# Seven products for eight in six of 22 up-projection chunks of a two-layer encoder

## The chip, the cores and the metric

The kernel runs as one program on one core of a Trainium2 chip. The metric is the device time of one execution in microseconds. The kernel before has a median of 1114.0 us in three runs (1113.79 to 1115.45). The profile is of one further execution.

## What is computed

The reference is an encoder of two layers on 512 tokens of width 1024: layer 0 mixes tokens with a gated linear attention, layer 1 with softmax attention, and each mixer is followed by a gated MLP. Only the MLP is touched here:

```python
def conv_ffn(h, w_up, w_conv, b_conv, w_down):      # h: 512 x 1024, w_up: 1024 x 5632, w_down: 2816 x 1024
    u = h @ w_up
    u = lax.conv_general_dilated(u, w_conv[:, None, :], window_strides=(1,), padding=[(1, 1)], ...) + b_conv
    val, gate = jnp.split(u, 2, axis=-1)
    return (jax.nn.silu(gate) * val) @ w_down
# per layer: x = x + mixer(rmsnorm(x)); x = x + conv_ffn(rmsnorm(x), ...)
```

## The kernel before

Features lie on the 128 partitions and the 512 tokens along a row. Every fp32 matrix product is done as three products of rounded parts: a weight or an input is split into a high part (ScalarE copies it to fp32r) and a low part (VectorE subtracts the high part), and TensorE adds high x high, high x low and low x high. So one strip of weights costs a ScalarE copy into a `wh` tile and a VectorE subtraction into a `wl` tile, besides its transfer into a `raw` tile by SyncE's queue.

**The up projection** runs over 22 chunks `m` in a layer. A chunk has two output tiles (`t` = 0 for the value, 1 for the gate); each tile takes 8 blocks of the input times 3 matmuls of 128x512 from one half of the chunk's strip. `act_up` then scales the sums by the norm's row `R` (VectorE, `u<-up,R`), runs the convolution (one ScalarE and two VectorE instructions on `y` for each tile), the SiLU and the product of value and gate.

**The down projection** is done partly by seven products for eight already. `prepare` (for each two chunks) makes sums and differences of the activations' half tiles (two GpSimd subtractions, two VectorE ones) and splits them into `gu` tiles; `summed` makes the sums of weight blocks on VectorE; `down_part`, run after chunks 9 and 17, issues for each of four strips seven products of 12 matmuls of 128x256 and puts partial sums in each other's places by ScalarE copies from PSUM to PSUM. One of the four weight pieces of such a strip gets its low part by a GpSimd DMA that accumulates (`wl<-raw`, L189). The last chunks' activations are multiplied plainly (`PLAIN`).

**What sets the order.** A scheduler takes the instructions by the order in which the program writes them, and engines then run their own queues strictly in order. `Weights` makes pieces ahead of their use (`ahead`); `wh` and `wl` have 3 tiles each, `raw` has 2, and single tiles serve some pieces of the summed strips (`ring`, `sq`). The pool `g` of 22 pairs of tiles holds, in this stage, the `gu` tiles and the weights' sums.

Of the kernel before, what the change touches and what calls it, by code (L numbers as in the profile page):

```python
# [45 lines left out]
DOWN_AFTER = {9: 0, 17: 1}  # L46

# [9 lines left out]
def hybrid_encoder_kernel(  # L57
# [54 lines left out]
    class Weights:  # L112
# [7 lines left out]
        def add(self, src, strips=None, pieces=2):  # L120
            for i in strips or range(src.shape[0]):
                self.todo += [(src, i, h) for h in range(pieces)]
                if pieces > 2:
                    self.sums[id(src), i] = {}

        def make(self, key):
# [8 lines left out]
            if (id(src), i) in self.sums:  # L135
                self.made[id(src), i, h] = self.summed(self.raw[id(src), i], self.sums[id(src), i], h)
                return
# [10 lines left out]
        def summed(self, raw, sums, h):  # L148
# [3 lines left out]
            if h == 0:  # L152
                sums["e"] = e = big(F32, "sum")
                with tc.issue_after(self.last.ins) if self.last else ExitStack():
                    dve.tensor_tensor(e[:, :S], a21, a22, ALU.add)
                    dve.tensor_tensor(a21, a21, a11, ALU.add)
                r = raw[:, : 2 * S]
            elif h == 1:
                e = sums["e"]
                dve.tensor_tensor(e[:, S:], e[:, :S], a11, ALU.add)  # L160
                r = e
            elif h == 2:
                r = raw[:, 2 * S :]
            else:
                e = sums["e"]
                r = tmp("sq", "sum4")
                dve.tensor_tensor(r, e[:, S:], a12, ALU.add)
                hi, lo = (sp.tile([P, S], F32R, tag="sq", bufs=3, name=nm(n)) for n in ("wh4", "wl4"))
                act.activation(hi, r, AF.Copy)
                self.last = dve.tensor_tensor(lo, r, hi.bitcast(F32), ALU.subtract)  # L170
                return hi, lo
# [49 lines left out]

    def add_ffn(layer):
        first = 0
        for m, part in DOWN_AFTER.items():
            W.add(up[layer], range(first, m + 1))
            W.add(down_w[layer], range(part * NQ, (part + 1) * NQ), 4)
# [3 lines left out]
        W.add(up[layer], range(first, FC))  # L230
        W.add(down_w[layer], range(NPART * NQ, down_w[layer].shape[0]))
# [531 lines left out]
    def ffn(layer, norm, cw, nxt):  # L763
        w_dn = down_w[layer]

        ahead = {(m + i // 2, i % 2): n for m in DOWN_AFTER for i, n in ((-1, 2), (0, 2), (1, 5))}
        plain = {}
        down = []
        quads = {}

        def act_up(m):

            res, pss = [], []
            for t in range(2):
# [3 lines left out]
                if t == 0 and m in DOWN_AFTER:  # L778
                    down.append(down_part(DOWN_AFTER[m], m))
                    next(down[-1])  # L780
# [4 lines left out]
            for t in range(2):  # L785
                ps = pss[t]
                cc = ((layer * 2 + t) * FC + m) * 4
                w = lambda i: cw[:, cc + i : cc + i + 1]
                u = tmp("u", "u")
                dve.tensor_tensor(u, ps, norm.R, ALU.mult)  # L790
# [35 lines left out]


        PLACE = {1: (0, S), 7: (0, 0), 6: (1, S), 5: (1, 0), 2: (2, 0), 4: (2, S), 3: (3, 0)}

        def down_part(part, m):  # L830
# [3 lines left out]
            src = w_dn  # L834
            pairs = [quads.pop(part * NQ + i) for i in range(NQ)]
            st = [{} for _ in range(NQ)]
            pieces = {}

            def product(n, i, dst, start):
                h, o = PLACE[i]  # L840
                if (n, h) not in pieces:
                    pieces[n, h] = W.piece(src, part * NQ + n, h, 3)
                wh, wl = pieces[n, h]
                for j in range(NQ):
                    sl = slice(o + j * P, o + (j + 1) * P)
                    mh, ml = pairs[j][i]
                    for a, (w, m) in enumerate(((wh, mh), (wh, ml), (wl, mh))):
                        mm(dst, w[:, sl], m, start=start and j == 0 and a == 0, stop=j == NQ - 1 and a == 2,  # L848
                           skip_group_check=True)
                W.flush()  # L850

            def begin(n):
                r = st[n]
                r[1] = bank("acc", "r1")
                product(n, 1, r[1][:, :H], True)
# [5 lines left out]
            for n in range(NQ):  # L861
                r, c, d = st[n], x[2 * n], x[2 * n + 1]
                r1, r2 = r[1][:, :H], r[2][:, :H]
                product(n, 6, r2, False)
# [3 lines left out]
                product(n, 7, r4, True)  # L868
                product(n, 2, r1, False)
                product(n, 5, r2, False)  # L870
# [3 lines left out]
                product(n, 4, r3, False)  # L874
# [6 lines left out]
                product(n, 3, r2, False)  # L881
                dve.tensor_tensor(c[:, H:], c[:, H:], r2, ALU.add)
                if n == 1 and m < 2 * NQ * NPART:
                    prepare(m // 2, *late)
# [13 lines left out]
        last = late = None  # L898
        for m in range(FC):
            y = act_up(m)  # L900
            if m >= 2 * NQ * NPART:
                t = big(F32R, "gu")
                split(y, t)
                plain[m] = (t[:, :S], t[:, S:])
            elif m % 2 == 0:
                last = y
            elif m not in DOWN_AFTER:
                prepare(m // 2, last, y)
            if m in DOWN_AFTER:
                late = last, y  # L910
                for _ in down[-1]:
                    pass
        cur, open_ = None, {}
# [248 lines left out]
def _layout(inputs):  # L1162
# [53 lines left out]
    a["w_up"] = con(up.transpose(0, 4, 2, 3, 1, 5).reshape(2, FC, P, 4 * S))  # L1216
    dn = i["ffn_w_down"].reshape(2, FC, P, KC, P)
# [29 lines left out]
```

## Time and profile before

| | before |
|---|---|
| median of 3 runs | 1114.0 us |
| profiled execution: time, span | 1113.87 us, 1112.2 us |
| busy TensorE, VectorE, ScalarE, GpSimd | 1105.3, 797.4, 562.3, 117.7 us |
| granted TensorE clock | 0.999 |
| first weight load of the up projection, layer 0 and layer 1 | 225.6 us, 754.5 us after the start |

The profiled execution took 1.67 us more than its span from first to last instruction. An engine's row reads: line of the kernel, engine, operation, tile written and tiles read, their shapes, count, then busy time in all and the mean of one in ns. In rows of the timeline the first two numbers are start and duration in us. PE is TensorE, PEld its weight loads, DVE VectorE, ACT ScalarE, POOL GpSimd, SP SyncE.

### The profile page before, as it was taken

Reading aid. Unit: us, or ns where it says so; the run is one execution under the profiler, and the core shown is the slowest. Engines: PE = TensorE matmul, PEld = TensorE weight load, DVE = VectorE, ACT = ScalarE, POOL = GpSimd, SP = SyncE. Lnnn points to the kernel's source line nnn. Section 1 sums busy time; section 2 is a strip of 40 time slices with the busy share of each in tenths; the row PEclk is TensorE's granted clock in tenths of the full one; section 3 lists DMA queues with packets and bytes.
Section 4 is the critical chain, followed back from the end, with each engine's and each line's share of the span. In section 5 each row is a group of like instructions: output and inputs, shape, how many; then the busy total and the mean of one; then the engine's idle time right before and its main releaser. Section 6 shows DMA issues by size and latency. Waiting matters only on the chain.

```text
span 1112.2 us, 14752 instructions
## 1 busy us (share of the span) xinstructions
PE 1105.3 (99%) x5780; PEld 947.4 (85%) x5780; DVE 797.4 (72%) x1217; ACT 562.3 (51%) x870; POOL 117.7 (11%) x126
## 2 busy tenths in 40 slices
PE   9999999999999999999999999999999999999998
PEld 7888888888889988898888888788888998889887
DVE  6785785667889577875664578766788957797572
ACT  5565343444556444653464777644455644465340
POOL 0100122001001000100004333000100100010000
PEclk9999999999999999999999999999999999999999
DMA  6322122232226423363247765423222642336322
GB/s 230 138 89 100 71 95 77 76 114 76 76 86 175 158 76 113 98 169 114 98 128 188 177 185 154 153 76 104 86 77 81 172 164 76 114 96 168 116 76 76
DMA packets 31413, 130.52 MB, mean 117 GB/s; under 512 B 3824, under 2 KB 4336, under 8 KB 20976
## 3 DMA queue, kind: packets, MB, share of 16 engines
q1 hardware_dynamic: 21072, 102.16, 26.5%
q0 software_dynamic: 5376, 18.88, 8.5%
q10 hardware_dynamic: 4896, 8.55, 2.1%
q8 instruction: 45, 0.74, 0.3%
q14 instruction: 24, 0.20, 0.1%
HBM read 100.21 MB, written 2.10 MB: 92 GB/s over the span
## 4 chain that ended last, share of the span: by engine, by line
PE 96%; ACT 1%; DMA 1%; DVE 1%; issue 0%; POOL 0%; ACTq 0%; SPq 0%; DVEq 0%
PE r L848 14%; PE up L351 14%; PE up L350 14%; PE up L352 14%; PE op L408 8%; PE vg L382 8%; PE dn L350 2%; PE dn L352 2%; PE dn L351 2%; PE o L676 1%; PE A L350 1%; PE av L382 1%; PE A L351 1%; PE A L352 1%; PE pt L1109 1%; PE q L350 1%
## 5 line engine op out<-in xcount | busy, mean ns | idle before, releaser
L350 PE MATMUL up<-xhl,wh 128*128 128x512 f32 x704 | 274.4, 390 | 0.0
L351 PE MATMUL up<-xhl,wh 128*128 128x512 f32 x704 | 274.0, 389 | 0.0
L352 PE MATMUL up<-xhl,wl 128*128 128x512 f32 x704 | 273.9, 389 | 0.0
L199 ACT ACTIVATE wh<-raw 128x1024 fp32r<-128x1024 f32 x132 | 139.4, 1056 | 212.1 <-PE up L351 108.2
L200 DVE TENSOR_TENSOR wl<-raw,wh 128x1024 fp32r<-128x1024 f32 x132 | 161.2, 1221 | 41.0 <-ACT wh L199 40.7
L352 PEld LDWEIGHTS up<-xhl,wl 128*128 128x128 f32 x704 | 132.2, 188 | 27.5
L350 PEld LDWEIGHTS up<-xhl,wh 128*128 128x128 f32 x704 | 132.2, 188 | 27.3
L351 PEld LDWEIGHTS up<-xhl,wh 128*128 128x128 f32 x704 | 132.2, 188 | 26.9
L848 PE MATMUL r<-gu,wh 128*128 128x256 f32 x640 | 116.4, 282 | 0.0
L848 PEld LDWEIGHTS r<-gu,wh 128*128 128x128 f32 x640 | 99.7, 191 | 0.3
L790 DVE TENSOR_TENSOR u<-up,R 128x512 f32<-128x512 f32 x88 | 60.2, 686 | 54.3 <-PE up L352 54.3
L848 PE MATMUL r<-gu,wl 128*128 128x256 f32 x320 | 90.4, 283 | 0.0
L792 ACT ACTIVATE y<-u,cw 128x512 f32<-128x512 f32 x88 | 71.1, 811 | 33.2 <-DVE u L790 33.0
L382 PE MATMUL vg<-wh,xhl 128*128 128x512 f32 x256 | 80.0, 390 | 0.7 <-ACT wh L199 0.4
L408 PE MATMUL op<-oT,wh 128*128 128x512 f32 x256 | 71.8, 394 | 0.5 <-ACT p L1073 0.5
L794 DVE SCALAR_TENSOR_TENSOR y<-u,cw,y 128x511 f32<-128x511 f32 x88 | 65.8, 749 | 2.0
L793 DVE SCALAR_TENSOR_TENSOR y<-u,cw,y 128x511 f32<-128x511 f32 x88 | 65.5, 745 | 1.2 <-ACT y L792 1.2
L796 ACT ACTIVATE y<-y 128x512 f32<-128x512 f32 x44 | 27.8, 633 | 72.6 <-DVE y L794 72.4
L848 PEld LDWEIGHTS r<-gu,wl 128*128 128x128 f32 x320 | 61.1, 191 | 0.0
L189 POOL DMA_DIRECT2D wl<-raw x32 | 28.5, 890 | 299.4 <-ACT wl L142 114.7
L382 PEld LDWEIGHTS vg<-wh,xhl 128*128 128x128 f32 x256 | 47.9, 188 | 11.3 <-ACT wh L199 0.8
L408 PEld LDWEIGHTS op<-oT,wh 128*128 128x128 f32 x256 | 47.3, 188 | 11.0 <-ACT p L1073 0.9
(232 smaller groups left out, 1931.8 us busy)
## 6 DMA issues: line engine op xcount, KB each, us to landing
raw<-in_w_up_dram SPq DMA_DIRECT2D x42, 1024.0 KB, 4.9
raw<-in_w_down_dram SPq DMA_DIRECT2D x22, 1024.0 KB, 4.8
wl<-raw POOLq DMA_DIRECT2D x32, 512.0 KB, 4.6
raw<-in_w_vg_dram SPq DMA_DIRECT2D x6, 1024.0 KB, 4.8
ring<-p ACTq DMA_DIRECT2D x22, 256.0 KB, 3.1
raw<-in_w_kq_dram SPq DMA_DIRECT2D x4, 1024.0 KB, 4.8
raw<-in_w_gout_dram SPq DMA_DIRECT2D x4, 1024.0 KB, 4.9
raw<-in_w_aout_dram SPq DMA_DIRECT2D x16, 256.0 KB, 4.9
```

The lines of the kernel that those rows point to most:

```text
L199: act.activation(hi[:, sl], r[:, sl], AF.Copy)
L200: dve.tensor_tensor(lo[:, sl], r[:, sl], hi[:, sl].bitcast(F32), ALU.subtract)
L350: mm(ps, wh, mh, start=start, stop=False)
L351: mm(ps, wh, ml, start=False, stop=False)
L352: return mm(ps, wl, mh, start=False, stop=stop)
L382: mm(ps[j][:, :width], hl[k][i == 2][:, j * P : (j + 1) * P], (wl if i == 1 else wh)[:, sl], start=k == 0 and i == 0, stop=k == KC - 1 and ...
L408: mm(pss[ng][n], wt[:, sl], mv, start=k == 0 and i == 0, stop=k == KC - 1 and i == 2)
L790: dve.tensor_tensor(u, ps, norm.R, ALU.mult)
L792: act.activation(y, u, AF.Identity, scale=w(1), bias=w(3))
L793: dve.scalar_tensor_tensor(y[:, 1:], u[:, : S - 1], w(0), y[:, 1:], ALU.mult, ALU.add)
L794: dve.scalar_tensor_tensor(y[:, : S - 1], u[:, 1:], w(2), y[:, : S - 1], ALU.mult, ALU.add)
L848: mm(dst, w[:, sl], m, start=start and j == 0 and a == 0, stop=j == NQ - 1 and a == 2, skip_group_check=True)
```

## The change

Six chunks in each layer (`SEVEN`: 4, 6, 12, 14, 18 and 20) compute their two output tiles by seven products of 12 matmuls of 128x256 in the place of two tiles of 24 matmuls of 128x512. The 1024 input features are taken as four pairs of blocks, the 512 tokens as two halves, and the chunk's strip as four quarters (odd or even blocks, gate or value). The sums of the weights' quarters are made by GpSimd for these chunks (`by` is `pool`); for the down strips they stay on VectorE, but the order of the sums and their places change, so that no tile of the pool `g` is needed. `prepare_input`, once a layer and for one pair of blocks after each of the chunks 0 to 3, makes the sums of the input's half tiles and their splits. The activations of two chunks are now `held` until both are there, and `prepare` comes after a down part, not in its midst.

```diff
+SEVEN = (4, 6, 12, 14, 18, 20)
...
-        def summed(self, raw, sums, h):
+        def summed(self, raw, h, by):
             a21, a11, a12, a22 = (raw[:, n * S : (n + 1) * S] for n in range(4))
             if h == 0:
-                sums["e"] = e = big(F32, "sum")
+                r = tmp("t", "sum")
                 with tc.issue_after(self.last.ins) if self.last else ExitStack():
-                    dve.tensor_tensor(e[:, :S], a21, a22, ALU.add)
-                    dve.tensor_tensor(a21, a21, a11, ALU.add)
+                    by.tensor_tensor(r, a21, a11, ALU.add)
+                    by.tensor_tensor(a21, a21, a22, ALU.add)
+                hi, lo = pair("wh", 3, F32R, "wh"), pair("wl", 3, F32R, "wl")
+                for sl, y in ((slice(0, S), r), (slice(S, 2 * S), a11)):
+                    act.activation(hi[:, sl], y, AF.Copy)
+                    dve.tensor_tensor(lo[:, sl], y, hi[:, sl].bitcast(F32), ALU.subtract)
+                return hi, lo
+            if h == 1:
+                by.tensor_tensor(a11, a21, a11, ALU.add)
...
             else:
-                dve.tensor_tensor(r, e[:, S:], a12, ALU.add)
+                by.tensor_tensor(r, a11, a12, ALU.add)
...
+    def add_up(layer, chunks):
+        for m in chunks:
+            W.add(up[layer], (m,), 4 if m in SEVEN else 2, pool)
...
+        ahead.update({(m - 1, t): 2 for m in SEVEN for t in range(2)})
...
+        def seven_up(m):
+            pieces = {}
+            go = lambda *a: product(pieces, up[layer], m, inputs, *a)
+            r1, r2 = (bank("acc", n)[:, :H] for n in ("r1", "r2"))
+            go(1, r1, True)
+            act.activation(r2, r1, AF.Copy)
+            r4 = bank("pt", "r4")[:, :H]
+            go(7, r4, True)
+            go(6, r2, False)
+            r3 = bank("s", "r3")[:, :H]
+            act.activation(r3, r2, AF.Copy)
+            go(2, r1, False)
+            go(5, r2, False)
+            c, d = tmp("u", "u"), tmp("u", "u")
+            act.activation(d[:, H:], r2, AF.Copy)
+            dve.tensor_tensor(c[:, :H], r1, norm.R[:, :H], ALU.mult)
+            go(4, r3, False)
+            dve.tensor_tensor(d[:, H:], d[:, H:], r4, ALU.add)
+            go(3, r2, False)
+            act.activation(d[:, :H], r3, AF.Copy)
+            dve.tensor_tensor(d[:, :H], d[:, :H], r4, ALU.add)
+            dve.tensor_tensor(c[:, H:], r2, norm.R[:, H:], ALU.mult)
+            yield c
+            dve.scalar_tensor_tensor(d, d, -1.0, norm.R, ALU.mult, ALU.mult)
+            yield d
...
+        def prepare_input(p):
+            y1, y2, q = (tmp("t", n) for n in ("x1", "x2", "q"))
+            for i, y in enumerate((y1, y2)):
+                act.activation(y, x[2 * p + i], AF.Copy, scale=norm.weight(2 * p + i))
+            b11, b12, b21, b22 = y1[:, :H], y1[:, H:], y2[:, :H], y2[:, H:]
+            pool.tensor_tensor(q[:, :H], b22, b12, ALU.subtract)
+            pool.tensor_tensor(b12, b11, b12, ALU.subtract)
+            t = [big(F32R, "xt") for _ in range(2)]
+            split(b12, t[0], 0, H)
+            dve.scalar_tensor_tensor(q[:, H:], b12, -1.0, b22, ALU.mult, ALU.subtract)
+            split(q, t[1])
+            dve.scalar_tensor_tensor(b21, q[:, H:], -1.0, b21, ALU.mult, ALU.subtract)
+            split(b21, t[0], H, H)
...
-                if n == 1 and m < 2 * NQ * NPART:
-                    prepare(m // 2, *late)
...
+        held = []
         for m in range(FC):
+            held.append(act_up(m))
+            if m < KC // 2:
+                prepare_input(m)
             if m in DOWN_AFTER:
                 for _ in down[-1]:
                     pass
+            if m % 2 == 0:
+                continue
+            if m < 2 * NQ * NPART:
+                prepare(m // 2, *held)
...
+            held = []
```

How the instructions move is seen at three places of layer 0. The first is GpSimd's queue over chunks 10 to 15. Before, it holds the two subtractions of `prepare` for each two chunks (`q` and `y`) and nothing between them:

```order
L810 TENSOR_TENSOR q_3470<-y_3458,y_3384 128x256
L811 TENSOR_TENSOR y_3384<-y_3384 128x256
L810 TENSOR_TENSOR q_3634<-y_3622,y_3548 128x256
L811 TENSOR_TENSOR y_3548<-y_3548 128x256
L810 TENSOR_TENSOR q_3799<-y_3787,y_3713 128x256
```

Now the same queue, from the last of chunk 12's weight sums on (`raw_3599` is chunk 12's strip, `raw_3797` chunk 14's; `y_3582` and `y_3665` are the activations of chunks 10 and 11):

```order
L172 TENSOR_TENSOR sum_3699<-raw_3599 128x512
L194 DMA wl_3696<-raw_3599 128x1024
L866 TENSOR_TENSOR q_3677<-y_3665,y_3582 128x256
L158 TENSOR_TENSOR sum_3799<-raw_3797 128x512
L867 TENSOR_TENSOR y_3582<-y_3582 128x256
L159 TENSOR_TENSOR raw_3797<-raw_3797 128x512
L166 TENSOR_TENSOR raw_3797<-raw_3797 128x512
L172 TENSOR_TENSOR sum_3925<-raw_3797 128x512
L194 DMA wl_3922<-raw_3797 128x1024
```

Four sums of 128x512 and one DMA have come in for each of the six chunks, and the first sum for chunk 14 stands between the two subtractions of `prepare` for chunks 10 and 11.

The second place is ScalarE's queue while TensorE runs chunk 12. Before (`gu` tiles are splits of `prepare`, `wh` tiles weight strips for later chunks):

```order
L792 ACTIVATE y_3464<-u_3462,cw 128x512
L796 ACTIVATE y_3464<-y_3464 128x512
L803 ACTIVATE gu_3474<-y_3458 128x512
L199 ACTIVATE wh_3561<-raw_3516 128x1024
L803 ACTIVATE gu_3473<-y_3384 128x512
L803 ACTIVATE gu_3475<-q_3470 128x512
```

Now (`r_3693`, `r_3694`, `r_3750` are chunk 12's PSUM banks r1, r2, r3; `u_3781` its second result):

```order
L848 ACTIVATE y_3671<-u_3669,cw 128x512
L820 ACTIVATE r_3694<-r_3693 128x256
L204 ACTIVATE wh_3752<-raw_3732 128x1024
L852 ACTIVATE y_3671<-y_3671 128x512
L825 ACTIVATE r_3750<-r_3694 128x256
L859 ACTIVATE gu_3681<-y_3665 128x512
L859 ACTIVATE gu_3680<-y_3582 128x512
L829 ACTIVATE u_3781<-r_3694 128x256
L859 ACTIVATE gu_3682<-q_3677 128x512
```

Copies on which TensorE's next product waits (L820, L825, L829) now stand between instructions that wait for VectorE and GpSimd (`gu_3680` for the subtraction into `y_3582`).

The third is TensorE's queue in chunk 4, the first of the six. Before, a tile is 24 rows of one kind:

```order
L350 MATMUL up_2373<-xhl_1811,wh_2345 128x512
L351 MATMUL up_2373<-xhl_1811,wh_2345 128x512
L352 MATMUL up_2373<-xhl_1811,wl_2346 128x512
L350 MATMUL up_2373<-xhl_1817,wh_2345 128x512
L351 MATMUL up_2373<-xhl_1817,wh_2345 128x512
```

Now, where the products 7 (`r_2447`), 6 (`r_2422`) and 2 (`r_2421`) meet (`xt_2396` is the transformed input of the last pair of blocks, `up_2562` the first tile of chunk 5):

```order
L810 MATMUL r_2421<-xhl_1917,wl_2424 128x256
L810 MATMUL r_2447<-xt_2396,wh_2315 128x256
L810 MATMUL r_2422<-xt_2396,ring_2347 128x256
L810 MATMUL r_2421<-xhl_1991,wh_2423 128x256 x2
L810 MATMUL r_2421<-xhl_1991,wl_2424 128x256
L361 MATMUL up_2562<-xhl_1811,wl_2463 128x512
L359 MATMUL up_2562<-xhl_1817,wh_2462 128x512
L810 MATMUL r_2447<-xt_2396,wh_2315 128x256
L810 MATMUL r_2447<-xt_2396,wl_2316 128x256
L810 MATMUL r_2422<-xt_2396,ring_2347 128x256 x2
```

The last pair's part of products 7 and 6 stands behind most of product 2, and nine matmuls of chunk 5 stand within chunk 4. In layer 1 the three queues have the same order at these places.

More of the change, by code (lines that the diff above doesn't have):

```diff
@@ L135, in make @@
             if (id(src), i) in self.sums:
[L136 removed]
+                self.made[id(src), i, h] = self.summed(self.raw[id(src), i], h, self.sums[id(src), i])
                 return
@@ L224, in add_ffn @@
         for m, part in DOWN_AFTER.items():
-            W.add(up[layer], range(first, m + 1))
-            W.add(down_w[layer], range(part * NQ, (part + 1) * NQ), 4)
+            add_up(layer, range(first, m + 1))
+            W.add(down_w[layer], range(part * NQ, (part + 1) * NQ), 4, dve)
             at = len(W.todo) - 4 * NQ - 1
@@ L229, in add_ffn @@
             first = m + 1
-        W.add(up[layer], range(first, FC))
+        add_up(layer, range(first, FC))
         W.add(down_w[layer], range(NPART * NQ, down_w[layer].shape[0]))
```

94 lines of the change are left out of this document (47 added, 47 removed).

## The prediction

> **What bounds the kernel now.** I read the page first: who is busy, and whose work the chain that ended last consists of.
>
> ```profile
> PE 1105.3 (99%) x5780; PEld 947.4 (85%) x5780; DVE 797.4 (72%) x1217; ACT 562.3 (51%) x870; POOL 117.7 (11%) x126
> PE 96%; ACT 1%; DMA 1%; DVE 1%; issue 0%; POOL 0%; ACTq 0%; SPq 0%; DVEq 0%
> ```
>
> TensorE has hardly any idle time, and 96% of the chain is its own work, so fewer matmul cycles shorten the span if nobody else comes late. How near the others are is asked by stage: the table of windows gives, for each stretch, the busy time of PE, PEld, DVE, ACT and POOL.
>
> ```profile
> 270.20:292.00 21.80, 21.80 (x98) 18.06 (x97) 17.06 (x24) 10.57 (x14) 1.83 (x2) 1.00 0.27 100
> 398.20:420.00 21.80, 21.80 (x98) 18.06 (x97) 17.10 (x25) 10.61 (x15) 1.83 (x2) 1.00 0.26 89
> 337.60:376.30 38.70, 38.70 (x326) 38.70 (x325) 32.92 (x53) 23.78 (x35) 4.98 (x5) 1.00 0.60 172
> 503.50:525.30 21.80, 21.80 (x98) 18.04 (x97) 12.41 (x16) 6.74 (x9) 0.00 (x0) 1.00 0.25 82
> ```
>
> Two plain chunks take 21.8 us, of which VectorE is busy 17.1 us: 4.7 us are free. Late chunks (from 503.5) leave it 9.4 us.
>
> **What goes: TensorE.** A matmul's own row is longer than its pitch, since matmuls overlap; so I take the pitch from runs of one shape in the chain, 128x512 first, 128x256 second.
>
> ```profile
> 84.06 16.32 PE vg L382 x72
> 337.63 38.69 PE r L848 x324
> ```
>
> 16.32/72 = 0.227 us and 38.69/324 = 0.119 us. A plain chunk is 48 x 0.227 = 10.88 us (the 21.8 us of the windows for two), a chunk of seven products 84 x 0.119 = 10.03 us. Half of 0.227 is 0.113, so the smaller matmul gives back 5% of the 12.5%. The gain is **0.85 us a chunk, 5.1 us a layer, 10.2 us in all**: small against any wait.
>
> **What comes: VectorE, ScalarE, GpSimd.** Groups by shape, mean ns before the last bar:
>
> ```profile
> L200 DVE TENSOR_TENSOR wl<-raw,wh 128x1024 fp32r<-128x1024 f32 x132 | 161.2, 1221 | 41.0 <-ACT wh L199 40.7
> L790 DVE TENSOR_TENSOR u<-up,R 128x512 f32<-128x512 f32 x88 | 60.2, 686 | 54.3 <-PE up L352 54.3
> L794 DVE SCALAR_TENSOR_TENSOR y<-u,cw,y 128x511 f32<-128x511 f32 x88 | 65.8, 749 | 2.0
> L804 DVE TENSOR_TENSOR gu<-y,gu 128x512 fp32r<-128x512 f32 x44 | 30.3, 689 | 16.6 <-ACT gu L803 16.4
> L183 DVE TENSOR_TENSOR ring<-sum,ring 128x1024 fp32r<-128x1024 f32 x16 | 20.4, 1276 | 6.2 <-ACT ring L182 6.2
> L170 DVE TENSOR_TENSOR wl<-sum,wh 128x512 fp32r<-128x512 f32 x16 | 11.0, 688 | 1.5 <-ACT wh L169 1.0
> L882 DVE TENSOR_TENSOR x<-x,r 128x256 f32<-128x256 f32 x16 | 6.7, 418 | 4.0 <-PE r L848 3.3
> L820 DVE SCALAR_TENSOR_TENSOR y<-q,y 128x256 f32<-128x256 f32 x16 | 6.7, 418 | 0.0
> L199 ACT ACTIVATE wh<-raw 128x1024 fp32r<-128x1024 f32 x132 | 139.4, 1056 | 212.1 <-PE up L351 108.2 <-PE op L408 32.3 <-issue 18.3
> L792 ACT ACTIVATE y<-u,cw 128x512 f32<-128x512 f32 x88 | 71.1, 811 | 33.2 <-DVE u L790 33.0
> L857 ACT ACTIVATE r<-r 128x256 f32<-128x256 f32 x16 | 5.9, 368 | 10.4 <-PE r L848 10.4
> L315 ACT ACTIVATE xhl<-x,prm 128x512 fp32r<-128x512 f32 x32 | 22.9, 715 | 11.4 <-DVE x L888 3.5 <-PE op L408 2.8 <-DMA x<-in_xT_dram 1.9
> L810 POOL TENSOR_TENSOR q<-y,y 128x256 f32<-128x256 f32 x16 | 11.8, 737 | 319.1 <-DVE y L797 319.1
> L577 POOL TENSOR_TENSOR end<-ek,fk 128x384 f32<-128x384 f32 x8 | 8.4, 1073 | 101.9 <-DVE ek L574 101.9
> ```
>
> VectorE, for a chunk of seven: weights 688 + 688 + 1276 + 688 ns (the third piece's low part goes by DMA) for 2 x 1221, +0.90 us; results 4 x 418 + 749 for 2 x 686, +1.05 us. So +1.95 us, 19.0 of the 20.9 us that two chunks then last. `prepare_input` adds 4 x 418 + 689 = 2.36 us four times a layer. ScalarE gets three more copies of weights (some 2.9 us) and four copies of sums (1.5 us): 15 of 20.9 us, fits. The extra 0.2 us a strip of the reordered down sums, and `prepare` moved behind the down part, land where VectorE has room (5.8 of 38.7 us, then plain chunks) and cost nothing; the first would cost about 1 us a layer without that room.
>
> GpSimd gets four sums of 128x512 that no row shows. Bounds: 1.43 us (1073 x 512/384) and 3.2 us (twice the slowest add of 256 below, 1.61). I take 1.45, next to 2 x 737; so 5.8 us a chunk. Does that slow VectorE? One place before has both at work (timeline of POOL, then DVE):
>
> ```profile
> 344.84 0.73 POOL L810 TENSOR_TENSOR q<-y,y 128x256 f32<-128x256 f32 x1 [0.96 <-DVE y L797]
> 345.65 1.61 POOL L811 TENSOR_TENSOR y<-y 128x256 f32<-128x256 f32 x1
> 345.01 1.65 DVE L183 TENSOR_TENSOR ring<-sum,ring 128x1024 fp32r<-128x1024 f32 x1 [0.26 <-ACT ring L182]
> 346.58 0.96 DVE L879 TENSOR_TENSOR x<-x,r 128x256 f32<-128x256 f32 x1
> ```
>
> VectorE took 1.65 where 1.22 is usual for that shape and 0.96 where 0.42 is: 0.97 us lost to 1.47 us of GpSimd's adds, a ratio of 0.66. Bounds are 0 (the adds of most chunks met an almost idle VectorE) and 1. By 0.66, a pair of chunks needs 17.1 + 1.95 + 3.8 = 22.9 us of VectorE where TensorE takes 20.9. [...]
>
> **Where lateness meets TensorE.** Not at the weights at first: the timeline below has one `wl` ready at 273.0 for a tile two tiles later, about 8.8 us ahead. It is a chain across three engines that now stands in front of a copy (rows of DVE, POOL and ACT; a tile of TensorE ended at 270.86, just before the first):
>
> ```profile
> 270.92 0.69 DVE L790 TENSOR_TENSOR u<-up,R 128x512 f32<-128x512 f32 x1 [1.51 <-PE up L352]
> 271.79 1.23 DVE L200 TENSOR_TENSOR wl<-raw,wh 128x1024 fp32r<-128x1024 f32 x1 [0.18 <-ACT wh L199]
> 275.22 0.69 DVE L797 TENSOR_TENSOR y<-y,y 128x512 f32<-128x512 f32 x1 [0.76 <-ACT y L796]
> 275.99 0.74 POOL L810 TENSOR_TENSOR q<-y,y 128x256 f32<-128x256 f32 x1 [19.78 <-DVE y L797]
> 276.81 1.09 POOL L811 TENSOR_TENSOR y<-y 128x256 f32<-128x256 f32 x1
> 277.94 0.63 ACT L803 ACTIVATE gu<-y 128x512 fp32r<-128x512 f32 x1 [0.41 <-POOL y L811]
> ```
>
> The split `gu` of the pair before starts 7.1 us after the tile's end. In the new ScalarE queue the copy of r2 (L829 of the changed kernel) stands right behind that split, and product 3 waits for the copy; product 3 is due 6 x 1.43 = 8.6 us after the chunk's start. VectorE's queue has another `wl` ahead of the product of the y's, whose high part waits for product 7 (2.87 + 1.06 us), so that product starts at 5.1 instead of 4.36, the split at 7.8, and the copy ends at 7.8 + 0.63 + 0.37 = 8.8: a wait of about **0.25 us with nothing late**, and every microsecond by which VectorE lags is added. The sum by chunk, for one layer:
>
> - Chunks 6 and 14: 0.25 plus a lag. A pair needs 1.9 us more of VectorE than it lasts; I take two thirds, since a waiting TensorE gives time back: 1.5 us each.
> - Chunk 12: the sum for chunk 14 stands between the two subtractions: 0.25 + 1.45 = 1.7 us.
> - Chunk 4: ahead of the copy r2<-r1 stand a `wh`, a `y` and two scalings (1.06 + 0.81 + 2 x 0.72 + 0.37 = 3.7 us, due at 2.95): 0.7 us. The last pair's input then goes through two GpSimd subtractions, a split, the SiLU, a VectorE step and another split, to about 6.6 us, where TensorE wants it at 5.85: 0.75. The copy r3<-r2 stands behind `gu` and a `wh`, to 10.6, due at 9.25: 1.35. With 2.8 us and a lag of 1.2 (chunks 2 and 3 need 17.1 + 2 x 2.36 us of 21.8, and GpSimd's slowing): 4.0 us.
> - Chunks 18 and 20: no GpSimd subtraction in the chain and VectorE at 12.4 of 21.8 us: nothing.
> - Second down part: the DMA for its last strip's low part now stands behind two sums of chunk 18, which wait for that strip's transfer. By the same stage of the first down part:
>
> ```profile
> 354.23 0.88 POOL L189 DMA_DIRECT2D wl<-raw  x1 [6.97 <-ACT wl L179]
> 363.89 0.88 POOL L189 DMA_DIRECT2D wl<-raw  x1 [8.78 <-DVE sum L167]
> 370.62 0.69 DVE L878 TENSOR_TENSOR x<-x,r 128x512 f32<-128x512 f32 x1 [1.57 <-PE r L848]
> ```
>
> and of the transfers, with the median from issue to landing last:
>
> ```profile
> raw<-in_w_up_dram SPq DMA_DIRECT2D x42, 1024.0 KB, 4.9
> wl<-raw POOLq DMA_DIRECT2D x32, 512.0 KB, 4.6
> ```
>
> 354.23 + 4.6 lets the strip's transfer start, + 4.9 lands it at 363.7, + 2.9 for two sums, + 4.6 for the DMA is 371.2; its product is due at about 370.6: 0.6, with some slowing 0.8 us.
>
> Lost 4.0 + 1.5 + 1.7 + 1.5 + 0.8 = 9.5 us, gained 5.1: +4.4 us a layer, +8.8 in all. 1112.2 + 8.8 = 1121.0 us of span, and with the 1.7 us outside it (1113.87 - 1112.2) **1122.7 us**; that execution is 0.1 us below the median of 1114.0, so the same number stands for the median.
>
> **Rivals.**
> - *Faster (0.23).* GpSimd's sums fall into VectorE's free 4.7 us, so nothing lags, and the next strip's transfer is early, so its sum does not hold up chunk 12. Then only chunk 4's 2.8 us stay: 10.2 - 5.6 = 4.6 us gained, 1109.4; with chunk 4 hidden as well, 1103.8. For it: low ScalarE load, weights 8.8 us ahead. Against: the slowed rows at 345 us. It decides at waits of 0.85 us a chunk.
> - *No difference (0.15).* No lag, but the queues' order costs as worked out: 2.8 + 0.25 + 1.7 + 0.25 + 0.8 = 5.8 against 5.1, 1115.4.
> - *Much slower (0.17).* VectorE becomes the bound: at a ratio of 1 it needs 3.9 us more than the chunks last in four pairs a layer, and chunk 4's 2.8 and the down part's 0.8 stay: 19.2 - 5.1 = 14.1 a layer, 1142.
> - That the change doesn't do what it says: the queue has 84 matmuls of 128x256 for 48 of 128x512 in each of the 12 chunks; no chance is left for it.
>
> **The numbers.** My forecast has 0.45, as 1116.5 to 1132 us. About 0.2%, 2.2 us, is what a measurement of this kernel can tell from no change: faster 0.24, same 0.15, slower 0.61. The range from 1107 to 1138 leaves out the best of the first rival and the upper half of the last.
>
> **What would show it.** TensorE's busy time should fall by about 10 us while idle time appears on rows of `r` (L810), ended by its ScalarE copies L820, L825 and L829, most in chunks 4 and 12; `wl` and `ring` rows of VectorE should be longer than 1.22 us beside GpSimd's sums; sums of 512 should last 1.45 us or more. I am wrong if TensorE has no idle time at L810 (faster), or if it waits at `up` tiles for `wl`: then VectorE is the bound and the loss is larger.

## The result and the profile after

| | before | after |
|---|---|---|
| median of 4 runs | 1113.89 us | 1146.94 us |
| lowest to highest | 1113.46 to 1115.45 us | 1145.75 to 1147.76 us |
| profiled execution: time, span | 1113.87, 1112.2 us | 1147.76, 1146.0 us |

The ratio is 1.0293 (95% interval 1.0275 to 1.0311): slower, as forecast, but by 33.1 us and not by 8.7, and above the range. The page of the changed kernel, busy times and then the chain that ended last:

```profile
PE 1110.6 (97%) x6212; PEld 967.6 (84%) x6212; DVE 863.5 (75%) x1333; ACT 630.2 (55%) x1022; POOL 210.0 (18%) x202
PE 75%; DVE 11%; issue 5%; ACT 4%; POOL 3%; DMA 2%; ACTq 0%; POOLq 0%; DVEq 0%; SPq 0%
```

TensorE is busy 5 us longer, though it has 10 us less to do, and a quarter of the chain is now others' work. Its waits in the up projection (who waited for what, us in all, times, longest), of which the kernel before had none:

```profile
PE r L810 <- ACT r L820: 8.3, 6, 1.8
PE up L359 <- ACT wh L204: 7.3, 2, 3.8
PE r L810 <- ACT u L829: 3.7, 2, 1.9
PE r L810 <- DVE xt L860: 3.6, 2, 1.8
```

Where they lie is seen when each layer is cut at the first matmuls of its stages (times in us from the timelines; "forecast" is the length before with the prediction's terms for that stretch):

| stretch of a layer | before | after, layer 0 | after, layer 1 | forecast |
|---|---|---|---|---|
| chunks 0 to 9, up to the first down part | 104.8 | 118.4 | 119.5 | 108.6 |
| first down part | 45.6 | 45.6 | 45.6 | 45.6 |
| chunks 10 to 17 | 81.6 | 83.5 | 83.4 | 83.1 |
| second down part | 45.6 | 45.9 | 47.1 | 46.4 |
| chunks 18 to 21 | 43.5 | 42.2 | 41.9 | 41.8 |

Of the 33.8 us by which the span grew, 30.8 lie in these stretches; 1.8 lie ahead of them and 1.2 between the layers, where the kernel was not changed. Four rows came out within 0.8 us. The first, with chunks 4 and 6, is off by 9.8 and 10.9 us. The windows of that place in layer 0, two chunks each (busy PE, PEld, DVE, ACT, POOL, then clock, DMA):

```profile
250.00:272.00 22.00, 21.74 (x97) 17.67 (x96) 18.83 (x29) 12.65 (x20) 6.60 (x7) 1.00 0.28 94
272.00:294.00 22.00, 14.05 (x73) 11.89 (x72) 20.37 (x24) 13.90 (x23) 12.21 (x11) 0.77 0.27 75
294.00:316.00 22.00, 20.16 (x132) 18.28 (x131) 20.30 (x30) 13.43 (x21) 5.37 (x5) 1.00 0.46 132
```

In the second window VectorE is busy 20.4 of 22 us, TensorE 14.1, and the granted clock is 0.77. The timeline of chunk 4 (rows of VectorE and GpSimd, then TensorE):

```profile
269.76 1.73 POOL L158 TENSOR_TENSOR sum<-raw 128x512 f32<-128x512 f32 x1
271.45 0.73 POOL L890 TENSOR_TENSOR x<-x 128x256 f32<-128x256 f32 x1
272.22 1.50 DVE L893 SCALAR_TENSOR_TENSOR q<-x,x 128x256 f32<-128x256 f32 x1 [1.87 <-POOL x L890]
273.51 1.36 POOL L166 TENSOR_TENSOR raw<-raw 128x512 f32<-128x512 f32 x1
273.64 1.78 DVE L163 TENSOR_TENSOR wl<-sum,wh 128x512 fp32r<-128x512 f32 x1
274.95 1.62 POOL L172 TENSOR_TENSOR sum<-raw 128x512 f32<-128x512 f32 x1
275.35 1.77 DVE L853 TENSOR_TENSOR y<-y,y 128x512 f32<-128x512 f32 x1
277.38 0.68 DVE L860 TENSOR_TENSOR xt<-q,xt 128x512 fp32r<-128x512 f32 x1
278.11 0.38 PE L810 MATMUL r<-xt,wh 128*128 128x256 f32 x1 [1.77 <-DVE xt L860]
282.37 0.80 PE L359 MATMUL up<-xhl,wh 128*128 128x512 f32 x1 [3.76 <-ACT wh L204]
285.21 2.29 PE L810 MATMUL r<-xt,ring 128*128 128x256 f32 x9 [1.62 <-ACT r L820]
```

Three VectorE instructions of some 0.42, 0.69 and 0.69 us take 1.50, 1.78 and 1.77 beside GpSimd's. The first of them has also waited 1.87 us for GpSimd's subtraction L890, which stands behind the first sum of weights. The input's last splits come after these three, and TensorE waits 1.77 us; ScalarE's copy of chunk 5's weights (`wh`, L204) comes after those, and TensorE waits 3.76. From 280.1 us on its matmuls run at half clock: the first 128x512 row is 0.80 us long, not 0.39.

### The profile page after: what moved, and what is told of

It is laid out like the page before. It is cut to its first block, busy times and chain, and to the rows that moved or that the text cites. A ratio compares the mean times of both kernels' runs of the same rounds, so it can differ in the third digit from the quotient of the medians.

```text
span 1146.0 us, 16132 instructions
## 1 busy us (share of the span) xinstructions
PE 1110.6 (97%) x6212; PEld 967.6 (84%) x6212; DVE 863.5 (75%) x1333; ACT 630.2 (55%) x1022; POOL 210.0 (18%) x202
## 4 chain that ended last, share of the span: by engine, by line
PE 75%; DVE 11%; issue 5%; ACT 4%; POOL 3%; DMA 2%; ACTq 0%; POOLq 0%; DVEq 0%; SPq 0%
PE r L810 17%; PE vg L391 8%; PE op L417 8%; PE up L359 7%; PE up L360 7%; PE up L361 7%; PE dn L360 2%; PE dn L361 2%; PE dn L359 2%; DVE wl L205 1%; DVE y L849 1%; DVE gu L860 1%; DVE y L853 1%; DVE u L798 1%; PE o L685 1%
## 5 line engine op out<-in xcount | busy, mean ns | idle before, releaser
L359 PE MATMUL up<-xhl,wh 128*128 128x512 f32 x512 | 200.7, 392 | 7.3 <-ACT wh L204 7.3
L361 PE MATMUL up<-xhl,wl 128*128 128x512 f32 x512 | 199.5, 390 | 0.6 <-DVE wl L205 0.6
L360 PE MATMUL up<-xhl,wh 128*128 128x512 f32 x512 | 199.9, 391 | 0.0
L204 ACT ACTIVATE wh<-raw 128x1024 fp32r<-128x1024 f32 x108 | 114.0, 1056 | 146.1 <-PE up L360 51.7
L205 DVE TENSOR_TENSOR wl<-raw,wh 128x1024 fp32r<-128x1024 f32 x108 | 131.8, 1220 | 44.2 <-ACT wh L204 43.7
L359 PEld LDWEIGHTS up<-xhl,wh 128*128 128x128 f32 x512 | 96.4, 188 | 27.1 <-ACT wh L204 7.8
L361 PEld LDWEIGHTS up<-xhl,wl 128*128 128x128 f32 x512 | 96.2, 188 | 21.3 <-DVE wl L205 1.4
L360 PEld LDWEIGHTS up<-xhl,wh 128*128 128x128 f32 x512 | 96.5, 188 | 19.0
L194 POOL DMA_DIRECT2D wl<-raw x44 | 39.2, 890 | 287.1 <-ACT wl L145 76.3
L810 PE MATMUL r<-xhl,wh 128*128 128x256 f32 x288 | 56.5, 294 | 4.1 <-ACT u L829 3.7
L798 DVE TENSOR_TENSOR u<-up,R 128x512 f32<-128x512 f32 x64 | 43.5, 683 | 17.5 <-PE up L361 17.5
L859 ACT ACTIVATE gu<-y 128x512 fp32r<-128x512 f32 (+1 forms) x60 | 33.9, 572 | 41.2 <-POOL y L867 19.3
```

Source lines behind the costliest of these rows:

```text
L204: act.activation(hi[:, sl], r[:, sl], AF.Copy)
L205: dve.tensor_tensor(lo[:, sl], r[:, sl], hi[:, sl].bitcast(F32), ALU.subtract)
L359: mm(ps, wh, mh, start=start, stop=False)
L360: mm(ps, wh, ml, start=False, stop=False)
L361: return mm(ps, wl, mh, start=False, stop=stop)
```

## The experiments

A comparison is with the kernel before on the same chip (1113.4 to 1113.7 us) or with the changed kernel (1146.9 us).

### Which part of the change costs

**Only chunks 18 and 20.**

```diff
-SEVEN = (4, 6, 12, 14, 18, 20)
+SEVEN = (18, 20)
```

> Only chunks 18 and 20 are done by seven products; the input's sums are still made after chunks 0 to 3. My theory is that the changed kernel's loss arises where the queues of VectorE and ScalarE are full (chunk 4 and, less, 6, 12 and 14) and that chunks 18 and 20, where VectorE was busy 12.4 of 21.8 us, give their 0.85 us each: 4 x 0.85 = 3.4 us off 1113.9, 1110.5 us, and no wait of TensorE in chunks 0 to 17 that the kernel before has not. The rival, that the input's sums alone overfill VectorE (17.1 + 2 x 2.36 of 21.8 us), expects waits in chunks 2 to 5 of 1 us a layer or more, 1113 us or above.

1119.4 us, ratio 1.0059 [1.0042, 1.0075]: my theory missed by 9 us, the rival held. The weights' wait in chunks 3 and 5 (four times in two layers), and a window there, with no seven-product chunk near:

```profile
PE up L361 <- DVE wl L205: 4.8, 4, 2.1
270.00:292.00 22.00, 19.88 (x88) 16.11 (x87) 20.46 (x33) 13.21 (x21) 3.62 (x4) 1.00 0.19 60
```

The input's sums alone take up nearly all of VectorE's time here and cost 2.4 us of waits a layer, more than two chunks gain. The second down part lost 2.7 and 1.1 us, at the DMA behind chunk 18's sums and at a copy.

**The input's sums a chunk earlier.**

```diff
-            if m < KC // 2:
-                prepare_input(m)
+            for p in {0: (0, 1), 1: (2,), 2: (3,)}.get(m, ()):
+                prepare_input(p)
```

> As the changed kernel, but the input's sums are made earlier: two pairs of blocks after chunk 0, the third after chunk 1, the fourth after chunk 2, so that the last is done a chunk (10.9 us) before chunk 4. If the fourth pair's lateness is what empties TensorE's queue in chunk 4 (waits of 1.77 us on its split and 3.76 us on the first weight strip of chunk 5, which stands behind it) and the clock halves because of these waits, some 5.5 us of waits and most of the 5 us of slow clock go in each layer: 1146.9 - 2 x 9 = 1129 us, no stretch at half clock. If VectorE's and ScalarE's total work over chunks 1 to 4 is the cause, the waits only change places and the time stays above 1140 us.

1147.5 us: the waits changed places (in layer 0 3.4 us at a `wl` of chunk 3, then 2.3, 0.6 and 3.4). So it is not the last pair's place, it is the work in chunks 1 to 5.

**No sums of weights.** `r = a21` and `r = a12` stand for the sums in the six chunks, and nothing is issued on GpSimd for them.

> As the changed kernel, but the four sums of weight quarters on GpSimd are left out in the six chunks (the splits read the quarters themselves, so the product is another); the input's sums stay. [...] If the input's sums and the order of the queues are the cause, chunk 4 keeps most of its 8.3 us and the time stays above 1130 us.

1123.8 us, under the 1130 us that the input's sums and the order of the queues, taken as the cause, were expected to keep it above. Chunks 6, 12 and 14 wait no more; chunk 4 and chunk 5's weights still do, 4.9 us in layer 0 and 4.8 in layer 1.

**No sums of the input.** `prepare_input` hands out the plain halves.

> As the changed kernel, but the input's sums and their splits are left out (products 4 to 7 read the halves of the plain split input, so the product is another); GpSimd's sums of weights stay. If the input's sums are what makes chunk 4 late, its waits fall from 8.3 us to about 2 and the clock stays up: 1146.9 - 2 x (6.3 + 5) = 1124 us. If GpSimd's weight sums are the cause, chunk 4 still waits over 5 us and the time is above 1138 us.

1131.2 us, between the two times expected. Chunk 4 still waits 6.1 us in layer 0 and 4.8 in layer 1, mostly at the copy L829, by the chain that the prediction has for chunk 12: a split of `prepare` waits for a GpSimd subtraction that stands behind a sum. Against the 1103.2 us that 12 gains of 0.85 us would give, a number that no run shows, the kernel with the input's sums alone is 20.6 us late, the one with the weights' sums alone 28.0, and the one with both 43.7. Both loads are real; each figure also holds what the new order of the queues costs, which no run has by itself.

### What GpSimd's sums do

**The weights' sums on VectorE,** nothing else changed.

```diff
-            W.add(up[layer], (m,), 4 if m in SEVEN else 2, pool)
+            W.add(up[layer], (m,), 4 if m in SEVEN else 2, dve)
```

> The changed kernel with one thing else: the weights' sums of the six chunks are on VectorE (48 x 0.69 = 33 us more of its own work). From the two kernels with the input's sums in chunk 0, of which the one with the sums on VectorE was 17 us faster at the same busy time of VectorE: 1146.9 - 17 to 20 = 1127 to 1130 us, the waits of chunks 12 and 14 below 0.9 us, those of chunks 2 to 5 still 3 us or more in a layer, with a stretch at half clock. If VectorE's load alone decided, 33 us more of it would make it slower than 1146.9 us.

1126.8 us, 20 us faster than the changed kernel, though VectorE has taken on 33 us of work. Chunk 12 waits no more; chunk 14 does, 1.7 and 1.5 us, more than expected. The same edit with the input's sums in chunk 0:

```diff
                     norm.tokens()
+                    for p in range(KC // 2):
+                        prepare_input(p)
```

> As the changed kernel, but all four pairs' input sums are made in chunk 0, where VectorE was idle for some 7 us of the 8 between 230.7 and 238.9 us of the profile before. If VectorE's time in chunks 2 to 5 is what is short, the time comes to that of the kernel without the input's sums, 1131 us (within 3), with the same waits in chunks 4, 6, 12 and 14. If the sums' place does not matter but their amount does, it stays at 1145 us.

> As the kernel with the input's sums in chunk 0, but the weights' sums of all six chunks are on VectorE. Two chunks then need 17.1 + 1.95 + 2.75 = 21.8 us of VectorE where TensorE takes 20.9. [...]

1138.7 us with GpSimd's sums, between its two times expected, and 1121.7 with VectorE's, 17 us less, though two chunks were reckoned to need 21.8 us of VectorE where TensorE takes 20.9. The busy times of the two, GpSimd's sums first, and of the kernel without sums:

```profile
PE 1109.4 (98%) x6212; PEld 967.4 (85%) x6212; DVE 861.8 (76%) x1333; ACT 628.5 (55%) x1022; POOL 211.7 (19%) x202
```

```profile
PE 1104.8 (99%) x6212; PEld 963.7 (86%) x6212; DVE 861.1 (77%) x1381; ACT 627.8 (56%) x1022; POOL 145.1 (13%) x154
```

```profile
PE 1102.7 (98%) x6212; PEld 962.9 (86%) x6212; DVE 836.4 (75%) x1333; ACT 628.1 (56%) x1022; POOL 142.1 (13%) x154
```

VectorE is as busy with GpSimd's help as without it. The groups of the four sums in the changed kernel (count, then busy and mean ns):

```profile
L172 POOL TENSOR_TENSOR sum<-raw 128x512 f32<-128x512 f32 x12 | 19.4, 1620 | 2.2 <-DVE wl L175 1.4
L158 POOL TENSOR_TENSOR sum<-raw 128x512 f32<-128x512 f32 x12 | 17.3, 1438 | 70.4 <-DMA raw<-in_w_up_dram 70.4
L159 POOL TENSOR_TENSOR raw<-raw 128x512 f32<-128x512 f32 x12 | 16.4, 1369 | 0.6
L166 POOL TENSOR_TENSOR raw<-raw 128x512 f32<-128x512 f32 x12 | 15.6, 1304 | 41.1 <-DVE wl L163 41.0
```

They are busy 68.7 us and lengthen VectorE's work by 863.5 - 836.4 = 27.1: 0.56 us for a sum that VectorE does in 0.69. Most of what the help saves is gone (by the first two busy times above, all of it), and the queue comes on top.

**GpSimd's sums made but not used,** first into new tiles, then (no tile held longer) all into one spare tile:

```diff
-                    by.tensor_tensor(r, a21, a11, ALU.add)
-                    by.tensor_tensor(a21, a21, a22, ALU.add)
+                    by.tensor_tensor(self.spare if by is pool else r, a21, a11, ALU.add)
+                    by.tensor_tensor(self.spare if by is pool else a21, a21, a22, ALU.add)
```

> The changed kernel with GpSimd's sums made at the same places but written to spare tiles that nothing reads (the splits read the quarters themselves, so the product is another). [...] Without the sums the kernel took 1123.8 us, with them 1146.9 us. If the wait for GpSimd's slow sums in its queue is the cost, the time is within 4 us of 1124 us; if the slowing of VectorE is, within 5 us of 1147 us; in between, the share is read off.

> The changed kernel with GpSimd's four sums made at the same places, all written to one spare tile that nothing reads; the splits read the quarters themselves (so the product is another). No instruction waits for a sum, and no tile is held longer, so what is left of the sums is their disturbance of VectorE. Without the sums the kernel took 1123.8 us, with them in use 1146.9 us. If the disturbance is the cost: 1140 us or more, and VectorE's busy time near the 863 us of the changed kernel. If waiting for the sums is the cost: 1128 us or less.

1156.9 and 1162.2 us, with VectorE busy 866.4 and 863.4 us: the sums disturb VectorE as much when nothing reads them. What waiting for their results costs can't be read from these times, since both are slower than with the sums in use. The second one's queue of GpSimd before chunk 12's wait, which grew to 5.7 us, shows why it is slower:

```profile
418.71 1.28 POOL L160 TENSOR_TENSOR spare<-raw 128x512 f32<-128x512 f32 x1 [8.70 <-DMA raw<-in_w_up_dram]
420.07 1.61 POOL L161 TENSOR_TENSOR spare<-raw 128x512 f32<-128x512 f32 x1
421.65 0.72 POOL L868 TENSOR_TENSOR q<-y,y 128x256 f32<-128x256 f32 x1
422.33 1.25 POOL L168 TENSOR_TENSOR spare<-raw 128x512 f32<-128x512 f32 x1
423.55 0.72 POOL L869 TENSOR_TENSOR y<-y 128x256 f32<-128x256 f32 x1
```

Without dependences to hold them, the scheduler put three sums ahead of `prepare`'s second subtraction, for which the chain to TensorE waits. In the changed kernel itself it is one sum, and that one waits for its strip (GpSimd, ScalarE, TensorE):

```profile
419.42 0.73 POOL L866 TENSOR_TENSOR q<-y,y 128x256 f32<-128x256 f32 x1 [7.25 <-DVE y L853]
421.04 1.29 POOL L158 TENSOR_TENSOR sum<-raw 128x512 f32<-128x512 f32 x1 [0.89 <-DMA raw<-in_w_up_dram]
422.28 0.73 POOL L867 TENSOR_TENSOR y<-y 128x256 f32<-128x256 f32 x1
419.36 0.63 ACT L859 ACTIVATE gu<-y 128x512 fp32r<-128x512 f32 x1 [1.10 <-DVE y L853]
423.04 0.63 ACT L859 ACTIVATE gu<-y 128x512 fp32r<-128x512 f32 x1 [3.05 <-POOL y L867]
423.58 0.36 ACT L829 ACTIVATE u<-r 128x256 f32<-128x256 f32 x1
424.00 0.50 PE L810 MATMUL r<-xhl,wh 128*128 128x256 f32 x2 [1.86 <-ACT u L829]
```

**`prepare`'s subtractions on VectorE,** the sums left on GpSimd:

```diff
-            pool.tensor_tensor(q[:, :H], b22, b12, ALU.subtract)
-            pool.tensor_tensor(b12, b11, b12, ALU.subtract)
+            dve.tensor_tensor(q[:, :H], b22, b12, ALU.subtract)
+            dve.tensor_tensor(b12, b11, b12, ALU.subtract)
```

> The changed kernel with the two subtractions of prepare on VectorE (2 x 0.42 us for two chunks, 13 us in all); GpSimd keeps the weights' sums, whose place in its queue they no longer share. If that queue is what delays chunk 12 (the subtraction behind a sum, the split behind the subtraction, the copy L829 behind the split), its wait of 1.85 us falls below 0.5 us, chunk 6 gains too, and the time is 1136 to 1142 us though VectorE has more to do. If the slowing of VectorE beside GpSimd's sums is what delays it, the wait of chunk 12 stays over 1.2 us and the time within 4 us of 1147 us.

1137.0 us, as the queue's theory expected, and chunk 12 waits no longer. Chunk 6 did not gain as expected (1.5 us in layer 0, 2.3 in layer 1), and chunk 14's wait rose from 0.7 to 1.7. ScalarE at chunk 12's wait:

```profile
416.51 0.63 ACT L859 ACTIVATE gu<-y 128x512 fp32r<-128x512 f32 x1 [1.10 <-DVE y L853]
417.43 0.63 ACT L859 ACTIVATE gu<-y 128x512 fp32r<-128x512 f32 x1 [0.29 <-DVE y L867]
417.97 0.37 ACT L829 ACTIVATE u<-r 128x256 f32<-128x256 f32 x1
```

From the first split to the copy it takes 1.5 us, where it took 4.2 in the changed kernel. Chunk 12's wait was the queue. Chunk 4's stays (3.5 + 2.1 + 1.5 us), and the longest of the three is for a `wl` of VectorE, whose queue again waits 1.9 us for the subtraction L890 behind a sum. Of the 20 us between GpSimd's sums and VectorE's (1146.9 and 1126.8), this edit takes away 10.

### The half clock

The edit puts matmuls of 128x512, whose result nobody reads, where chunks 4 and 5 waited:

```diff
             go(7, r4, True)
+            if m == 4:
+                fill(norm.hl, 8)
...
+            if m == 5:
+                fill(norm.hl, 12)
```

> The changed kernel with 20 more matmuls of 128x512 in each layer whose result nobody reads (8 after product 7 of chunk 4, 12 ahead of chunk 5): 20 x 0.227 = 4.5 us a layer of work that is useless but for keeping TensorE busy where it waited 8 us. If the half clock is the answer to those waits, the stretches of half clock go or shrink, the matmuls fill time that was lost anyway, and the time falls to 1137 to 1143 us. If the half clock has another cause, the matmuls add up to 9 us: 1150 us or more.

1149.9 us, which settles nothing: the order of TensorE's queue changed with them, a wait of 4.8 us opened behind them, and two stretches of 10.24 us at half clock stayed, with two of 3.41 us more. What the half clock costs is read from the changed kernel's trace instead, below.

### Versions

All but the one with chunks 18 to 21 have the weights' sums on VectorE. With the input's sums ahead in chunk 0 as above:

> Seven products in chunks 18 and 20 alone, the input's sums in chunk 0, the weights' sums on VectorE (4 x 0.69 = 2.75 us a chunk, where 9.4 of 21.8 us were free). No wait of TensorE in chunks 0 to 5, none in the second down part for the transfer behind GpSimd's sums: 4 x 0.85 us off 1113.4, 1110.0 us. If the wait in the second down part comes from the strip's late transfer and not from GpSimd's queue, it stays at 1 to 2 us in a layer and the time is 1112 to 1113 us; if chunk 0 has no room for the input's sums, over 1114 us.

1117.3 us. The rest is clean, but chunk 0 took 7.6 us longer in the two layers: the new splits stood ahead of the normed input's, and TensorE waited five times for those, 0.3 to 1.1 us each, with 6.8 us of half clock after it in layer 1. So they went behind them:

```diff
+                    with tc.issue_after(norm.last.ins):
+                        for p in range(KC // 2):
+                            prepare_input(p)
...
-            dve.tensor_copy(self.rtok, r)
+            self.last = dve.tensor_copy(self.rtok, r)
```

> Six chunks, weights' sums on VectorE, and the input's sums put behind the last of the normed input's splits in chunk 0 (after the copy of the norm's column), so that they fill the gap of VectorE before chunk 0's results and hold up none of TensorE's operands. The kernel with the input's sums in chunk 0 and VectorE's sums lost some 9 us there, in waits and half clock, of its 1121.7: 1112.5 us expected, 1110 to 1115. If chunks 0 to 2 then lack VectorE's time for weights, TensorE waits for wl tiles and the time stays above 1117 us.

> As the last, with seven products in chunks 18 and 20 alone. The kernel with the same and the input's sums ahead of the last splits took 1117.3 us, of which 7.6 us were lost in chunk 0: 1109.7 us expected (1113.4 - 4 x 0.85 = 1110.0). If the input's sums cost in chunks 0 to 2 wherever they are put, 1113 us or more.

With chunks 18 and 20 alone 1110.1 us, ratio 0.9973 [0.9964, 0.9982], as expected: no wait is left in the up projection. With all six 1121.6 us, 9 above the expectation. By stages, against 12 gains of 0.85 us, chunks 0 to 9 lost 5.7 and 5.2 us (waits of 2.8 and 2.9 us before copies in chunk 4), chunks 10 to 17 2.5 and 1.8. Some 3 us more were lost in the attention, which the change does not touch. VectorE's rows around chunk 4 are not slowed here (0.68 us for a `wl` of 128x512), and it has still no room: it is busy 20.6, 19.9 and 20.1 of 22 us in three windows. A full window alone does no harm, though. The version with 18 and 20 has the same one (second line), with TensorE busy throughout, and 19.0 us behind it:

```profile
248.00:270.00 22.00, 22.00 (x99) 18.21 (x97) 20.64 (x33) 12.09 (x18) 1.83 (x2) 1.00 0.28 96
248.00:270.00 22.00, 22.00 (x99) 18.22 (x98) 20.60 (x30) 12.44 (x17) 1.83 (x2) 1.00 0.26 96
```

> Seven products in chunks 6, 14, 18 and 20, VectorE's sums, the input's sums in VectorE's gap in chunk 0. With 18 and 20 alone it took 1110.1 us; 6 and 14 stand four chunks clear of any other, and with all six they waited 0.2 to 0.6 us each: 4 x (0.85 - 0.4) = 1.8 us less, 1108.3 us, at best 1106.7 us. If VectorE's 21.8 us of work in 20.9 us of chunk costs even alone, each waits 0.85 us or more: 1110 us or above.

1114.8 us, a ratio of 1.0009 [1.0000, 1.0018]; chunks 0 to 9 took 0.6 and 0.8 us longer than without chunk 6, chunks 10 to 17 0.4 us less than without chunk 14. The rest is again the attention: 177.6 us against 174.7 in the profile of the version with 18 and 20. There TensorE waits 2.2 us for a DMA (`ring<-p`, at L1174), and 3.41 us at half clock follow; the version with 18 and 20 has neither.

> Seven products in chunks 18, 19 and 20, the rest as with 18 and 20 alone (1110.1 us). If VectorE's room decides (3 x 4.7 us more beside 9.4 of 21.8 us free), 2 x 0.85 us less: 1108.4 us. If two such chunks in a row collide in the one ring tile and the banks, as with GpSimd's sums in 19 to 21 (waits of 1.1 and 2.2 us), 1110 us or more.

1110.7 us, ratio 0.9969 [0.9959, 0.9980]: no wait, and a time that can't be told from that with 18 and 20. By the profiles the last stretch is 0.6 us shorter in each layer, and 1.4 us more ahead of layer 0's up projection, where the two kernels are the same, hide it.

> Seven products in chunks 18, 19, 20 and 21 alone, the input's sums in chunk 0, the weights' sums of chunk 18 on VectorE, of 19 to 21 on GpSimd. If VectorE's room decides (12.4 of 21.8 us, plus 2 x 1.95 and some 4 us of GpSimd's disturbance for two chunks, 20 of 20.1 us), nothing or little waits: 8 x 0.85 = 6.8 us off 1113.4, 1106.6 to 1108 us. If two chunks in a row collide in the one ring tile and in the PSUM banks, TensorE waits 1 us or more at each of chunks 19 to 21, and the time is above 1110 us.

1132.9 us. Chunk 0 lost time as with the input's sums ahead of the last splits, and chunks 19 to 21, with GpSimd's sums, waited 0.9 to 2.2 us at a time before copies; against four gains of 0.85 us their stretch lost 6.4 and 7.5 us.

> Seven products in chunks 14, 18 and 20, VectorE's sums, the input's sums in VectorE's gap in chunk 0. With 6, 14, 18 and 20 the stretch with chunk 14 was 0.4 us shorter than with 18 and 20 alone, the one with chunk 6 0.6 to 0.8 us longer: 1110.1 - 0.8 = 1109.3 us expected, a ratio of 0.9960 to 0.9970. If chunk 14 costs as much as it gains, 1110.1 us or more.

1109.8 us, ratio 0.9967 [0.9955, 0.9980], the lowest of all, though its interval overlaps those of chunks 18 and 20 alone and of 18 to 20. Chunk 14 alone gains 0.4 us a layer. Its page:

```profile
PE 1101.0 (99%) x5996; PEld 953.9 (86%) x5996; DVE 839.8 (76%) x1327; ACT 607.4 (55%) x974; POOL 140.3 (13%) x148
PE 95%; ACT 1%; DMA 1%; DVE 1%; POOL 0%; issue 0%; ACTq 0%; SPq 0%; DVEq 0%
```

## Why the prediction was wrong in size

**Right, or near.** The gain of 0.85 us a chunk: chunks 18 to 21 came to 41.9 us in layer 1, where 41.8 were forecast. GpSimd's sum at 1.45 us: 1.30 to 1.62, mean 1.43. Chunk 12's chain: 1.7 us forecast, 1.86 and 1.84 measured, by the very instructions named, and gone when the subtractions left that queue; that the size fits so well is partly luck, since 0.89 us of the chain is GpSimd's wait for the strip, which was not in the sum. Nothing at chunks 18 and 20. The second down part: 0.8 forecast, 0.3 and 1.5. Chunk 6: 1.5 forecast, 1.84 and 1.83, though at the copy L820. Chunk 14: 1.5 forecast, 0.7.

**Mis-sized: chunk 4, 4.0 us forecast.** Chunks 0 to 9 hold 20.7 of the 24.2 us by which the forecast fell short. The rows have 7.9 and 8.1 us of waits for chunk 4, with the next chunk's first matmul. The copy L820 was 0.7 and is 1.6; the input's last pair 0.75 and is 2.3 with the weights' low part; the copy L825 1.35 and is 0.3 to 0.6. The largest, 3.6 to 3.8 us at chunk 5's weights, was not in the sum. The step that failed is "not at the weights at first": the lead of 8.8 us was read from plain chunks, and the lag of 1.2 us for "17.1 + 2 x 2.36 us of 21.8" took an engine with no idle time for one that is just in time. VectorE's queue also waits for others (1.87 us for L890); with 20.4 of 22 us busy it could not catch up, and the input's sums alone emptied the lead (first experiment). The "much slower" case, VectorE as the bound, came nearest, 1142 us with a chance of 0.17, and its upper half was left out of the range. It got there by another way, with 3.9 us in each of four pairs of chunks, where chunks 12 and 14 lost 1.9 and 0.7.

**Left out: the clock.** In the up projections of the changed kernel 23.9 us run at half clock, TensorE busy in 6.35 + 5.04 + 3.40 us of it: matmuls of 128x256 start 0.213 us apart there and 0.119 at full clock, so some 44% of that, about 6.5 us by this estimate, is lost on top of the waits. No term and no rival had it, since the trace of before showed only 1.00 in these stages; a sum of waits up to 4 us should have asked what a wait does to the clock.

**Right in kind, too large: GpSimd's disturbance.** It was forecast at 3.8 us a chunk (0.66 x 5.8) and is 2.3 (27.1 us over 12 chunks). The 0.66 set the 0.97 us that VectorE lost against the 1.47 us that two such adds usually take; the rows have them at 0.73 + 1.61 = 2.34 us, slowed themselves, which makes 0.41. Measured in the same way over all sums it is 0.39 (27.1 of 68.7 us). Single encounters were worse: the three rows of chunk 4 lost 3.25 us beside 4.26 us of sums. No run shows the ratio of 1 from which the much slower case was worked out: it is 0.39 over all sums and 0.76 in that place of chunk 4. What slows VectorE's rows beside GpSimd's, and why the mean is lower than in chunk 4, was not shown.

**Open.** Waits, clock and gain do not add up to the last microsecond: a wait's row begins where the matmul before it ends, and rows of 128x256 last 0.28 us at a pitch of 0.12, so each wait costs about 0.16 us more than it shows. The attention differs by up to 4 us between these kernels. In the traces the late ones have a wait for the DMA `ring<-p` and half clock behind it (1.2 and 3.41 us with all six chunks on VectorE's sums, 2.1 and 6.83 us with 18 to 21); why that transfer comes late was not tried.

## What to carry to other kernels

Before giving an engine work that "fits", look for its fullest stretch and for what must be early there: an engine that is busy 90% of one stretch did no harm here, but over several stretches in a row it had no room to catch up, and a lead of 8.8 us was used up within a few chunks. VectorE was hardly spared here by handing its sums to GpSimd (0.56 of 0.69 us a sum came back); price such work as VectorE's, and look at what else stands in GpSimd's queue. Save matmuls where the other engines have room (here chunks 14 and 18 to 20), and put one-time preparation in a gap behind what TensorE waits for, not ahead of it.

## What the runs showed of the hardware

In the changed kernel a wait of TensorE could be followed by matmuls at half speed: behind the waits of 1.77 and 3.76 us in chunk 4 a row of 128x512 took 0.80 us, not 0.39. The granted clock changed in steps: its stretches at half lasted 3.41, 6.83 or 10.24 us in these runs, multiples of 3.41, and those of the changed kernel started at 280.08, 822.80 and 856.93 us, whole numbers of 3.41 us apart. Its windows on that grid, to within 0.05 us (busy PE first, the clock third from the right):

```profile
276.70:280.10 3.40, 0.50 (x2) 0.30 (x2) 3.40 (x7) 1.83 (x4) 0.00 (x0) 1.00 0.00 0
280.10:283.50 3.40, 1.13 (x2) 0.50 (x2) 3.09 (x6) 2.67 (x4) 0.95 (x1) 0.50 0.61 116
283.50:286.90 3.40, 1.78 (x9) 1.69 (x9) 2.81 (x3) 1.66 (x4) 1.84 (x2) 0.50 0.48 89
286.90:290.30 3.40, 3.40 (x18) 3.40 (x18) 2.89 (x6) 2.48 (x5) 1.40 (x3) 0.50 0.64 265
853.50:856.90 3.40, 1.57 (x13) 1.36 (x12) 3.37 (x5) 2.06 (x3) 0.00 (x0) 1.00 0.37 67
856.90:860.30 3.40, 3.40 (x18) 3.40 (x17) 2.58 (x4) 1.53 (x3) 1.34 (x2) 0.50 0.94 328
307.40:310.80 3.40, 1.89 (x16) 1.68 (x15) 3.37 (x5) 1.91 (x4) 0.00 (x0) 1.00 0.62 116
420.05:423.46 3.41, 2.08 (x18) 1.88 (x16) 1.09 (x2) 0.42 (x1) 2.52 (x4) 1.00 0.85 324
966.16:969.57 3.41, 1.58 (x14) 1.38 (x12) 1.11 (x2) 0.90 (x2) 2.94 (x3) 1.00 0.70 279
```

After a step with 0.50 or 1.57 us of work the next ran at half clock; after 1.89 or 2.08 us it stayed full. Steps of 1.13 and 1.78 us at half clock did not bring the full clock back, and one of 3.40 us did. So a wait of 1.83 us, at chunk 6, was followed by a half-clock step in layer 1, and one of 1.84 us by none in layer 0, where it spreads over two steps. How much work is enough stays open: the last line, chunk 12 of layer 1, has 1.58 us in a step with a wait of 1.84 us, and the clock stayed full.
